# A hybrid decoder trunk on one core: the feed-forward norm reordered, its weight applied at PSUM exit, its sums moved off GpSimd, and the residual spread over eight down blocks

## The chip, the core and the metric

The kernel runs on one core of a Trainium2 chip. A core has five engines that run their own instruction queues side by side: TensorE (PE, matrix products; the loads of its stationary operand are shown as PEld), VectorE (DVE), ScalarE (ACT), GpSimd (POOL) and SyncE (SP), which here issues every DMA, in order. SBUF is the on-chip memory, PSUM the accumulator memory of PE, in eight banks for each of 128 partitions. The metric is the device time of one execution, in microseconds (us).

## The reference

Two layers; x is 1024 tokens by 1024 features, float32. What concerns the change is the second half of each layer:

```
D_MODEL, SEQ, D_FF, CONV_W = 1024, 1024, 2816, 3
def rms_norm(x, g):
    return x * rsqrt(mean(x * x, -1) + EPS) * g

for layer in range(2):
    h = rms_norm(x, norm_mix_g[layer])
    mix = even_mixer(...) if layer == 0 else gla_mixer(...)   # ends in  ... @ w_out
    x = x + mix
    h = rms_norm(x, norm_ffn_g[layer])
    g = causal_dwconv(h @ w_gate, conv_w, conv_b)             # width 3 along the tokens
    x = x + (silu(g) * (h @ w_up)) @ w_down
```

## The kernel before

Every product in question is made in three passes of a reduced float32 format (`fp32r`): a value is split into a high part (ACT casts it) and a low part (DVE subtracts the cast from the value), and `PASSES` multiplies high by high, high by low and low by high. `split(dst, src)` (lines 83 to 86) is that pair of instructions, and its rows in the profile carry lines 85 and 86 wherever it is called.

The 1024 tokens are eight tiles of 128 (`NT`). The normed activations are kept transposed (features on the partitions) in `hq[g][half]`: g is the parity of the feature block of 128, half the half of the tokens (tiles 0 to 3, or 4 to 7).

**Output projection and norm.** `out_first` makes the first 512 output columns for all tiles. `out_second` then makes the other 512, tile by tile: it loads the row tile `xt` (the first half from `xd`, where `out_first` put it, the second from the layer's input), `out_half` runs 24 products into a PSUM tile (`po`), adds them to the second half of `xt` on DVE (line 331) and writes that half to `xd` (line 332). `norm_tile` (line 118) follows for the same tile: ACT squares the row with a sum (line 123), POOL makes the inverse root (lines 114 and 115), DVE scales the row by it and by the norm weight `gB`, a copy of the weight on every partition, into a separate tile `h` (line 126), PE transposes `h` in eight blocks into PSUM (`pt`, line 135), and the result is split into `hq`.

**The feed-forward products** (`ffn_up`, line 192) use Strassen's scheme in Winograd's form on blocks: a stream is two feature blocks of gate or of up, and has seven products, steps 1 to 7, instead of eight. Their right operands are `hq[0][0]`, `hq[1][0]`, `hq[1][1]`, `hq[0][1]` for steps 1 to 4 and `T3[0]`, `T3[1]`, `T3[2]` for 5 to 7: differences of token halves, made once a layer. They need a tile of the second half with the tile four places before it, so they are made when tiles 4 to 7 are normed (lines 129 to 153): ACT copies the transposed blocks to `b`, POOL rebuilds the first half's values (`kept`, line 144), POOL and DVE make t1 to t4 (lines 145 to 148), and five splits follow. The left operands are sums of weight blocks, on POOL (`summed`, line 211), split like all others. The products go to PSUM tiles A, B and C (`pgA` for gate, `puA` for up, and so on); eight one-bank tiles (`m1`) are there. Steps 1 and 2 of the first two streams come first, then a loop over the streams makes steps 5, 6, 2, 7, the next stream's step 1, and 4 and 3. The depthwise convolution and SiLU follow on DVE and ACT, and the result goes to DRAM (`actd`).

**The down projection** (`ffn_down`, line 291) goes over blocks of two feature blocks (`FBLK`). Each block loads two activations and two weights into buffers of the pool `rawp` (four buffers of 512 KB for everything that is loaded raw), splits them, and runs 12 products of 512 columns for each token tile (`pd`, line 308); DVE adds them to the row tile `xs[n]` (line 318). The residual `xd` is loaded into the same pool and added (line 320) in one block of the eleven, for all eight tiles: `if fs[0] == NF // 4 * 2`, the sixth.

The order of each engine's instructions is fixed when the kernel is built: a planner takes the program in the order of the code and reorders each engine's queue by its own estimates of costs and due times. Buffers are given out tile by tile; an instruction that takes over a buffer waits for the last users of the old tile.

Of the kernel before, what the change touches and what calls it, by code (L numbers as in the profile page):

```python
# [51 lines left out]
def trunk(ctx: ExitStack, tc: tile.TileContext, a, out):  # L52
# [10 lines left out]
    small.tile([P, 8], F32, tag="pad", name="pad")  # L63
# [54 lines left out]
    def norm_tile(n, xt, gB, ps, pool, T3=None):  # L118


        h = pool.tile([P, D], F32, tag="h", bufs=2, name=f"h{n}")
# [3 lines left out]
        for _, c in HALVES:  # L125
            V.scalar_tensor_tensor(h[:, c], xt[:, c], r, gB[:, c], op0=ALU.mult, op1=ALU.mult)  # L126
        half, cols = n // 4, slice((n % 4) * P, (n % 4 + 1) * P)
        both = lambda t: [t[:, i, :, cols] for i in range(2)]
        if T3 and half:
            b = pool.tile([P, 2, 4, P], F32, tag="b", bufs=2, name=f"b{n}")  # L130
        for g in range(2):
            pt = ps.tile([P, 4, P], F32, tag="pt", name=f"pt{n}{g}")
            for j in range(4):
                k = 2 * j + g
                T.transpose(pt[:, j, :], h[:, k * P : (k + 1) * P], ident)  # L135
            if T3 and half:
                A.copy(b[:, g], pt)
            else:
                split(both(hq[g][half]), pt)
        if T3 and half:  # L140
            t1, t2, t3, t4 = (pool.tile([P, 4, P], F32, tag="tf", bufs=4, name=f"tf{n}{i}") for i in range(4))
            kept = [pool.tile([P, 4, P], F32, tag="kept", bufs=2, name=f"kept{n}{g}") for g in range(2)]
            for g in range(2):
                G.tensor_tensor(kept[g], *both(f32(hq[g][0])), op=ALU.add)
            G.tensor_tensor(t1, b[:, 0], kept[0], op=ALU.subtract)
            G.tensor_tensor(t3, b[:, 1], b[:, 0], op=ALU.subtract)
            V.tensor_sub(t2, b[:, 1], t1)
            V.tensor_sub(t4, kept[1], t2)
            split(both(T3[1]), t2)
            split(both(T3[0]), t1)  # L150
            split(both(T3[2]), t3)
            split(both(hq[0][1]), t4)
            split(both(hq[1][1]), b[:, 1])
# [38 lines left out]
    def ffn_up(l, T3, ps, pool):  # L192
# [6 lines left out]
        def stream(kind, f):  # L199
# [7 lines left out]
            sums, bank = {}, {}  # L207
# [16 lines left out]

            def step(p):
                L = parts_of(left(p), f"w{kind}{f}p{p}")
# [3 lines left out]
                if not more:  # L230
                    bank[b] = ps.tile([P, 512], F32, tag="m1", name=f"p{kind}{b}{f}")
# [20 lines left out]
            return step, out  # L252

        def conv(f, g2):
            ts = []
            for i in range(2):
                g = g2[:, i, :]
                t = pool.tile([P, S], F32, tag="t", bufs=3, name=f"t{f + i}")
                w = lambda j: cw[:, f + i, j : j + 1]
                A.activation(t, g, AF.Identity, bias=cb[:, f + i : f + i + 1], scale=w(2))  # L260
                V.scalar_tensor_tensor(t[:, 1:], g[:, : S - 1], w(1), t[:, 1:], op0=ALU.mult, op1=ALU.add)  # L261
                V.scalar_tensor_tensor(t[:, 2:], g[:, : S - 2], w(0), t[:, 2:], op0=ALU.mult, op1=ALU.add)  # L262
                A.activation(t, t, AF.Silu)  # L263
                ts.append(t)
            return ts
# [3 lines left out]
        for step, _ in (cur, nxt):  # L269
            step(1)  # L270
            step(2)
        for i, (kind, f) in enumerate(todo):
            step, out = cur
# [17 lines left out]
    def ffn_down(l, ps, pool, xs, final):  # L291
# [6 lines left out]
        def down(fs, last):  # L298
            acts = [act(f) for f in fs]
            wd = [load_w(a["w_down"][l, f], f"wd{f}") for f in fs]  # L300
            for n in range(NT):
# [15 lines left out]
                else:  # L317
                    V.tensor_add(xs[n], xs[n], flat(pd))  # L318
                    if fs[0] == NF // 4 * 2:
                        V.tensor_add(xs[n], xs[n], load_raw(xd[l][n], f"xd{l}{n}"))  # L320
# [7 lines left out]
    def out_half(l, half, wo, n, ps, xh):  # L328
        pd = ps.tile([P, 512], F32, tag="mm", name=f"po{half}{n}")
# [492 lines left out]
    for l in range(2):  # L822
# [59 lines left out]
def layouts(i):  # L882
# [21 lines left out]
    def ff(x):  # L904
# [8 lines left out]
        "norm_ffn_g": A["norm_ffn_g"],  # L913
# [37 lines left out]
```

## Time and profile before

| | us |
|---|---|
| median of 3 runs | 2363.51 (2362.66 to 2364.31) |
| profiled execution | 2365.36 |
| its span, first to last instruction | 2363.7 |
| PE busy | 2256.5 (95%) |
| DVE busy | 1388.8 (59%) |
| ACT busy | 890.2 (38%) |
| POOL busy | 486.9 (21%) |

The mean granted clock of PE is 0.979 of full speed. The first layer's second half of the output projection and its norm run from about 476 to 541 us of the span, gate and up from there to 972, down from 974 to 1223; the second layer's from about 1612, 1677 and 2110. A row of a timeline gives the start, the time from it to the end of the last instruction in the row, engine, line, operation, output and inputs, the count, and in brackets the idle time of the engine just before with what ended it. A row of groups gives a total and the mean in ns of one. A row of stretches gives each engine's busy time in the stretch.

### The profile page before, as it was taken

The numbers are of one execution on the slowest core, as the hardware profiler recorded it, in microseconds if no ns is written. First come the engines' busy times: TensorE is split into PE (matmuls) and PEld (weight loads), VectorE is DVE, ScalarE is ACT, GpSimd is POOL, SyncE is SP. The second block draws the span as 40 slices with busy tenths as digits, with TensorE's granted clock in tenths as the row PEclk, the third lists the DMA queues.
The fourth block names the chain that finished last, engine by engine and source line by source line (L and its number), as shares of the span: only waits on it lengthen the run. The fifth ranks groups of instructions, "written<-read, shape, count | busy, mean of one in ns | idle before, by whom it ended". The sixth has DMA issues, their size and how long they took to land.

```text
span 2363.7 us, 29172 instructions
## 1 busy us (share of the span) xinstructions
PE 2256.5 (95%) x11064; PEld 1912.0 (81%) x11064; DVE 1388.8 (59%) x2167; ACT 890.2 (38%) x1578; POOL 486.9 (21%) x535
## 2 busy tenths in 40 slices
PE   7999999988999999999999999999699999999999
PEld 7988877876888888787888888878588888878777
DVE  7666744458665655567664443244955655556674
ACT  5444554244443444511134333223444444442020
POOL 4333310036332332000000111001733323200000
PEclk9999999998999999999999999999799999999999
DMA  4122202341222222424232111454122222243241
GB/s 142 48 68 78 77 23 81 120 156 48 96 72 90 78 83 82 168 72 166 78 116 80 50 52 57 144 190 164 51 72 89 85 76 98 72 143 107 93 148 72
DMA packets 93309, 223.68 MB, mean 95 GB/s; under 512 B 10432, under 2 KB 35008, under 8 KB 93168
## 3 DMA queue, kind: packets, MB, share of 16 engines
q1 hardware_dynamic: 93168, 221.81, 28.1%
q8 instruction: 87, 1.43, 0.2%
q14 instruction: 54, 0.44, 0.1%
HBM read 167.18 MB, written 54.59 MB: 94 GB/s over the span
## 4 chain that ended last, share of the span: by engine, by line
PE 83%; DVE 8%; issue 3%; ACT 3%; DMA 2%; POOL 1%; SPq 0%; DVEq 0%; ACTq 0%; POOLq 0%
PE pd L308 19%; PE pgB L235 10%; PE puB L235 9%; PE po L171 6%; PE pgC L235 5%; PE pv L171 5%; PE puC L235 5%; PE pj L171 4%; PE pr L171 4%; PE pgA L235 2%; PE puA L235 2%; PE pk L183 2%; PE pq L183 2%; PE pu L171 1%; DVE T L86 1%
## 5 line engine op out<-in xcount | busy, mean ns | idle before, releaser
L308 PE MATMUL pd<-wd,act 128*128 128x512 f32 x2112 | 486.2, 392 | 14.5 <-ACT wd L85 9.7
L308 PEld LDWEIGHTS pd<-wd,act 128*128 128x128 f32 x2112 | 399.5, 189 | 100.4 <-ACT wd L85 14.7
L318 DVE TENSOR_TENSOR xr<-xr,pd 128x1024 f32<-128x1024 f32 x159 | 193.5, 1219 | 133.9 <-PE pd L308 133.3
L171 PE MATMUL po<-wo,hq 128*128 128x512 f32 x768 | 183.9, 394 | 2.2 <-ACT hq L349 1.3
L171 PEld LDWEIGHTS po<-wo,hq 128*128 128x128 f32 x768 | 141.7, 188 | 31.2 <-ACT hq L349 2.3
L171 PE MATMUL pv<-wv,hq 128*128 128x256 f32 (+2 forms) x960 | 155.5, 315 | 2.2 <-DVE gae L86 1.5
L171 PE MATMUL pj<-wq,hq 128*128 128x384 f32 x768 | 156.3, 351 | 1.3 <-ACT hq L85 1.3
L171 PEld LDWEIGHTS pv<-wv,hq 128*128 128x128 f32 x960 | 133.9, 191 | 11.0 <-DVE gae L86 1.7
L171 PEld LDWEIGHTS pj<-wq,hq 128*128 128x128 f32 x768 | 136.1, 195 | 2.0 <-ACT hq L85 1.7
L171 PE MATMUL pr<-wr,hq 128*128 128x512 f32 x384 | 97.9, 404 | 0.0
L287 DVE TENSOR_TENSOR t<-t,u 128x1024 f32<-128x1024 f32 x44 | 56.7, 1293 | 63.7 <-ACT u L248 63.7
L171 PEld LDWEIGHTS pr<-wr,hq 128*128 128x128 f32 x384 | 71.2, 188 | 14.5
L261 DVE SCALAR_TENSOR_TENSOR t<-g,cw,t 128x1023 f32<-128x1023 f32 x44 | 73.8, 1716 | 10.9 <-ACT t L260 10.9
L85 ACT CAST act<-ar 128x1024 fp32r<-128x1024 f32 x44 | 45.5, 1048 | 90.8 <-DMA ar<-actd 90.8
L135 PE MATMUL pt<-ident,h 128*128 128x128 f32 x256 | 40.8, 302 | 34.8 <-DVE h L126 26.0
L135 PEld LDWEIGHTS pt<-ident,h 128*128 128x128 f32 x256 | 33.0, 155 | 41.0 <-ACT h L123 16.1
L114 POOL TENSOR_SCALAR rn<-ssq 128x1 f32<-128x1 f32 x32 | 8.3, 261 | 264.8 <-ACT h L123 264.1
L263 ACT ACTIVATE t<-t 128x1024 f32<-128x1024 f32 x44 | 46.7, 1062 | 29.9 <-DVE t L262 29.8
L211 POOL TENSOR_TENSOR S2u<-S1u,ru 128x512 f32<-128x512 f32 x22 | 32.5, 1475 | 119.7 <-issue 113.0
L86 DVE TENSOR_TENSOR act<-ar,act 128x1024 fp32r<-128x1024 f32 x44 | 53.2, 1220 | 6.5 <-ACT act L85 6.4
L114 POOL TENSOR_SCALAR ro<-oss 128x1 f32<-128x1 f32 x32 | 9.8, 308 | 225.1 <-ACT og L765 225.1
L262 DVE SCALAR_TENSOR_TENSOR t<-g,cw,t 128x1022 f32<-128x1022 f32 x44 | 56.0, 1272 | 0.0
(920 smaller groups left out, 4716.9 us busy)
## 6 DMA issues: line engine op xcount, KB each, us to landing
rg<-in_w_gate SPq DMA_DIRECT2D x44, 512.0 KB, 3.6
ru<-in_w_up SPq DMA_DIRECT2D x44, 512.0 KB, 3.6
actd<-t SPq DMA_DIRECT2D x44, 512.0 KB, 2.6
ar<-actd SPq DMA_DIRECT2D x44, 512.0 KB, 4.2
xd<-xd SPq DMA_DIRECT2D x16, 512.0 KB, 4.3
x<-in_x SPq DMA_DIRECT2D x8, 512.0 KB, 5.3
xd<-xh SPq DMA_DIRECT2D x16, 256.0 KB, 2.0
xt<-xd SPq DMA_DIRECT2D x16, 256.0 KB, 3.1
```

Of the source, the lines that this page charges most:

```text
L85: (hi or A.copy)(dst[0], src)
L86: (lo or V.tensor_sub)(dst[1], src, f32(dst[0]))
L135: T.transpose(pt[:, j, :], h[:, k * P : (k + 1) * P], ident)
L171: T.matmul(o, L[i], R[jj][:, sl], start=(k == 0 and (ii, jj) == PASSES[0]), stop=(k == nk - 1 and (ii, jj) == PASSES[-1]))
L183: T.matmul(ps[h], L[i], hq[k % 2][h][:, jj, k // 2, :], start=(k == 0 and (ii, jj) == PASSES[0]), stop=(k == KD - 1 and (ii, jj) == PASSES ...
L235: T.matmul(o, L[ii][:, j * P : j * P + P], right[p][:, jj, j, :], skip_group_check=more, start=(not more and j == 0 and (ii, jj) == PASSES ...
L261: V.scalar_tensor_tensor(t[:, 1:], g[:, : S - 1], w(1), t[:, 1:], op0=ALU.mult, op1=ALU.add)
L262: V.scalar_tensor_tensor(t[:, 2:], g[:, : S - 2], w(0), t[:, 2:], op0=ALU.mult, op1=ALU.add)
L263: A.activation(t, t, AF.Silu)
L287: V.tensor_mul(ts[j], ts[j], out[:, j, :])
L308: T.matmul(pd[:, h, :], acts[k][:, i, n * P : (n + 1) * P], wd[k][h][jj], start=(k == 0 and (ii, jj) == PASSES[0]), stop=(k == len(fs) - 1 ...
L318: V.tensor_add(xs[n], xs[n], flat(pd))
```

## The change

`out_second` now takes the tiles in pairs, 0 4, 1 5, 2 3, 6 7; the row tiles of a pair are loaded into the buffers that later hold the gate and up outputs (tags `g` and `u`), and the scaled row overwrites the row tile (one `tensor_scalar` by the inverse root, no weight). The norm weight comes as one value for each partition and feature block (`gT`) and is applied when the transposed blocks leave PSUM: for tiles 0 to 3 by DVE, into `k`, which is kept for the partner tile and split into `hq`; for tiles 4 to 7 by eight multiplications on ACT, into `b`. t1 to t4 are made by DVE, and each is split at once. Tile 7's part after the scaling is handed to `ffn_up`, which calls it after steps 1 and 2 of the first stream and three early weight splits. The weight sums of the first two streams are made by DVE instead of POOL. `out_second` and `ffn_up` share one SBUF pool and one set of PSUM tiles: six `m1` (also for `po`) and two `pt`, which the transposes and the products A use. In the down projection, tile n's residual is added in block n + 1, counted from 0.

```
-    def norm_tile(n, xt, gB, ps, pool, T3=None):
+    def norm(n, xt, ps, h, gB=None):
         ssq = small.tile([P, 1], F32, tag="ssq", name=f"ssq{n}")
         A.activation(h, xt, AF.Square, accum_out=ssq)
         r = inv_rms(ssq, 1, D, f"rn{n}")
...
+        if gB is None:
+            h = xt
+            V.tensor_scalar(h, xt, r, None, op0=ALU.mult)
...
+        def turn(put):
             for g in range(2):
+                pt = ps.tile([P, 4, P], F32, tag="pt", name=f"pt{n}{g}")
+                for j in range(4):
+                    k = 2 * j + g
+                    T.transpose(pt[:, j, :], h[:, k * P : (k + 1) * P], ident)
+                put(g, pt)
+        return turn
...
             def summed(name, x, y, op):
-                sums[name] = pool.tile([P, 512], F32, tag="S", bufs=3, name=f"{name}{kind}{f}")
-                G.tensor_tensor(sums[name], x, y, op=op)
+                sums[name] = pool.tile([P, 512], F32, tag="S", bufs=4, name=f"{name}{kind}{f}")
+                (G if f else V).tensor_tensor(sums[name], x, y, op=op)
...
-                    bank[b] = ps.tile([P, 512], F32, tag="m1", name=f"p{kind}{b}{f}")
+                    bank[b] = ps.tile([P, 512], F32, tag="pt" if b == "A" else "m1", name=f"p{kind}{b}{f}")
...
-                t = pool.tile([P, S], F32, tag="t", bufs=3, name=f"t{f + i}")
+                t = pool.tile([P, S], F32, tag="t", bufs=4, name=f"t{f + i}")
...
-        for step, _ in (cur, nxt):
+        for step, _, _ in (cur, nxt):
             step(1)
             step(2)
+            if step is cur[0]:
+                for prep, p in ((nxt[2], 1), (nxt[2], 2), (cur[2], 5)):
+                    prep(p)
+                norm_end()
...
-                    if fs[0] == NF // 4 * 2:
+                    if fs[0] == FBLK * (n + 1):
                         V.tensor_add(xs[n], xs[n], load_raw(xd[l][n], f"xd{l}{n}"))
...
-    def out_second(l, w, x_in, g, T3, ps, pool):
+    def out_second(l, w, x_in, T3, ps, pool):
         wo = load_half(w[1], "wo1")
-        gB = load_g(pool, g, f"gBf{l}")
-        for n in range(NT):
-            xt = pool.tile([P, D], F32, tag="xt", bufs=2, name=f"xt{l}{n}")
-            Q.dma_start(xt[:, :512], xd[l][n][:, :512])
-            Q.dma_start(xt[:, 512:], x_in(n)[:, 512:])
-            out_half(l, 1, wo, n, ps, xt[:, 512:])
-            norm_tile(n, xt, gB, ps, pool, T3)
+        gT = small.tile([P, KD], F32, tag="gT", bufs=1, name=f"gT{l}")
+        Q.dma_start(gT, a["norm_ffn_gT"][l])
...
+        def temp(name):
+            return both(pool.tile([P, S], F32, tag="t", bufs=4, name=name))
+        def first(n, turn, k):
+            def put(g, pt):
+                gains = gT[:, g:KD:2, None].to_broadcast([P, 4, P])
+                V.tensor_tensor(k[:, g], pt, gains, op=ALU.mult)
+                split(place(hq[g][0], n), k[:, g])
+            turn(put)
+        def second(n, turn, k, b):
+            def put(g, pt):
+                for j in range(4):
+                    A.mul(b[:, g, j, :], pt[:, j, :], gT[:, 2 * j + g : 2 * j + g + 1])
+            turn(put)
+            t1, t2, t3, t4 = (F4(pool.tile([P, 512], F32, tag="S", bufs=4, name=f"tf{n}{i}")) for i in range(4))
+            V.tensor_sub(t1, b[:, 0], k[:, 0])
+            split(place(T3[0], n), t1)
+            V.tensor_sub(t2, b[:, 1], t1)
+            split(place(T3[1], n), t2)
+            V.tensor_sub(t3, b[:, 1], b[:, 0])
+            split(place(T3[2], n), t3)
+            V.tensor_sub(t4, k[:, 1], t2)
+            split(place(hq[0][1], n), t4)
+            split(place(hq[1][1], n), b[:, 1])
+        mine = {}
+        for i, pair in enumerate(((0, 4), (1, 5), (2, 3), (6, 7))):
+            xts = pool.tile([P, 2, S], F32, tag="gu"[i % 2], bufs=1, name=f"xt{l}{i}")
+            for j, n in enumerate(pair):
+                xt = xts[:, j]
+                Q.dma_start(xt[:, :512], xd[l][n][:, :512])
+                Q.dma_start(xt[:, 512:], x_in(n)[:, 512:])
+                out_half(l, 1, wo, n, ps, xt[:, 512:], "m1")
+                mine[n] = temp(f"n{n}")
+                turn = norm(n, xt, ps, mine[n].rearrange("p g a b -> p (g a b)"))
+                if n < 4:
+                    first(n, turn, mine[n])
+                elif n < 7:
+                    second(n, turn, mine[n - 4], mine[n])
+        return lambda: second(7, turn, mine[3], mine[7])
...
-            with tc.tile_pool(name=f"on{l}", bufs=1, reuse_waits="tile") as npool:
-                out_second(l, w_out, x_in, a["norm_ffn_g"][l : l + 1, :], T3, ps, npool)
             pss.close()
             with ExitStack() as st, tc.tile_pool(name=f"fu{l}", bufs=1, reuse_waits="tile") as fp:
-                ffn_up(l, T3, banks(st, m1=8), fp)
+                ps = banks(st, m1=6, pt=2)
+                norm_end = out_second(l, w_out, x_in, T3, ps, fp)
+                ffn_up(l, T3, ps, fp, norm_end)
```

More of the change, by code (lines that the diff above doesn't have):

```diff
@@ L124, in norm_tile @@
         r = inv_rms(ssq, 1, D, f"rn{n}")
[L125 to L139, printed above, removed]
@@ L140, in norm_tile @@
-        if T3 and half:
-            t1, t2, t3, t4 = (pool.tile([P, 4, P], F32, tag="tf", bufs=4, name=f"tf{n}{i}") for i in range(4))
-            kept = [pool.tile([P, 4, P], F32, tag="kept", bufs=2, name=f"kept{n}{g}") for g in range(2)]
-            for g in range(2):
[L144 to L153, printed above, removed]
+        if gB is None:
+            h = xt
+            V.tensor_scalar(h, xt, r, None, op0=ALU.mult)
+        else:
+            for _, c in HALVES:
+                V.scalar_tensor_tensor(h[:, c], xt[:, c], r, gB[:, c], op0=ALU.mult, op1=ALU.mult)
@@ new lines, in turn, with place, norm_tile @@
+        def turn(put):
+            for g in range(2):
+                pt = ps.tile([P, 4, P], F32, tag="pt", name=f"pt{n}{g}")
[4 more added lines that the diff above has]
+        return turn
+    def place(t, n):
+        return [t[:, i, :, (n % 4) * P : (n % 4 + 1) * P] for i in range(2)]
+    def norm_tile(n, xt, gB, ps, pool):
+        norm(n, xt, ps, pool.tile([P, D], F32, tag="h", bufs=2, name=f"h{n}"), gB)(
+            lambda g, pt: split(place(hq[g][n // 4], n), pt))
@@ L223, in left, with prep @@
                 return {1: A11, 2: A12, 4: A22}[p]
+            def prep(p):
+                made[p] = parts_of(left(p), f"w{kind}{f}p{p}")
             def step(p):
-                L = parts_of(left(p), f"w{kind}{f}p{p}")
+                if p not in made:
+                    prep(p)
+                L = made[p]
                 b = {2: "A", 5: "C", 3: "C"}.get(p, "B")
```

20 lines of the change are left out of this document (11 added, 9 removed).

## The prediction

> **What bounds the kernel now.** I read the page's busy shares and its chain first, to know whether TensorE (PE) is the bound; then the busy times by stretches, to find where PE is not busy; then the timelines of PE, VectorE (DVE) and the DMA queue (SP) in those stretches.
>
> ```profile
> PE 2256.5 (95%) x11064; PEld 1912.0 (81%) x11064; DVE 1388.8 (59%) x2167; ACT 890.2 (38%) x1578; POOL 486.9 (21%) x535
> PE 83%; DVE 8%; issue 3%; ACT 3%; DMA 2%; POOL 1%; SPq 0%; DVEq 0%; ACTq 0%; POOLq 0%
> ```
>
> PE sets the time nearly everywhere, so a change pays only where PE waits. Now the stretches:
>
> ```profile
> core 0: us, PE busy (x) PEld busy (x) DVE busy (x) ACT busy (x) POOL busy (x), PEclk, DMA share, GB/s
> 492.00:524.00 32.00, 32.00 (x166) 26.81 (x164) 18.19 (x25) 14.90 (x29) 10.32 (x15) 1.00 0.39 131
> 524.00:541.00 17.00, 4.05 (x16) 2.83 (x16) 17.00 (x18) 7.17 (x14) 13.06 (x10) 0.61 0.04 16
> 541.00:561.00 20.00, 13.65 (x53) 10.72 (x51) 19.21 (x19) 8.01 (x15) 11.98 (x8) 0.84 0.02 3
> 1081.00:1125.00 44.00, 39.21 (x160) 31.53 (x159) 36.40 (x35) 9.80 (x13) 0.00 (x0) 0.92 0.60 197
> 1661.00:1677.00 16.00, 3.80 (x15) 2.66 (x16) 16.00 (x17) 6.33 (x12) 12.07 (x10) 0.60 0.04 16
> 1677.00:1697.00 20.00, 13.85 (x52) 11.05 (x51) 19.21 (x19) 7.84 (x15) 12.15 (x8) 0.84 0.02 2
> ```
>
> From 524 to 561 PE is idle for 12.95 + 6.35 = 19.3 us while DVE has no idle time to speak of (17.00 of 17.00, 19.21 of 20.00). That is the end of the feed-forward norm. The second layer repeats it at 1661: 12.2 + 6.15 = 18.35 us in these two stretches. Around 1100, in the down projection, PE loses 4.8 us more. PE's own rows in the norm:
>
> ```profile
> 531.71 1.09 PE L135 MATMUL pt<-ident,h 128*128 128x128 f32 x4 [7.63 <-DVE h L126]
> 533.97 1.12 PE L135 MATMUL pt<-ident,h 128*128 128x128 f32 x4 [1.17 <-DVE h L126]
> 538.74 1.09 PE L135 MATMUL pt<-ident,h 128*128 128x128 f32 x4 [3.66 <-ACT T L85]
> 540.32 1.11 PE L135 MATMUL pt<-ident,h 128*128 128x128 f32 x4 [0.49 <-DVE h L126]
> 541.09 4.68 PE L235 MATMUL pgB<-hq,wg0p 128*128 128x512 f32 x12
> 548.35 2.88 PE L235 MATMUL puB<-hq,wu0p 128*128 128x512 f32 x12
> 560.30 5.32 PE L235 MATMUL pgC<-T,wg0p 128*128 128x512 f32 x12 [6.34 <-ACT wg0p L85]
> 966.36 3.02 PE L235 MATMUL puB<-hq,wu20p 128*128 128x512 f32 x12 [0.90 <-ACT u L245]
> 498.16 1.03 PE L135 MATMUL pt<-ident,h 128*128 128x128 f32 x8
> 498.95 5.70 PE L171 MATMUL po<-wo,hq 128*128 128x512 f32 x24
> ```
>
> The transposes of tiles 6 and 7 wait for their scaled rows, and the fifth product (pgC) for its weights, whose sum sat behind the tile work on POOL. The stalls also slow what follows: a group of twelve takes 4.68 and 5.32 us behind them and 2.88 otherwise (granted clock 0.61 and 0.84 in these stretches), 1.8 + 2.4 us lost. Sixteen transposes take 4.1 us there (1.09 + 1.12 + 1.09 + 0.77 to the next start); where PE is fed, eight take 0.8 us to the next start, so 2.5 us are lost. Together 19.3 + 4.2 + 2.5 = **26 us a layer** is the most that the norm can give back.
>
> Why DVE is late there:
>
> ```profile
> 536.47 1.58 POOL L145 TENSOR_TENSOR tf<-b,kept 128x512 f32<-128x512 f32 x1 [2.13 <-ACT hq L85]
> 538.01 1.71 POOL L146 TENSOR_TENSOR tf<-b 128x512 f32<-128x512 f32 x1
> 536.85 3.42 DVE L126 SCALAR_TENSOR_TENSOR h<-xt,rn,gBf 128x512 f32<-128x512 f32 x2
> 508.19 1.41 DVE L126 SCALAR_TENSOR_TENSOR h<-xt,rn,gBf 128x512 f32<-128x512 f32 x2 [1.16 <-POOL rn L115]
> 540.19 1.75 DVE L148 TENSOR_TENSOR tf<-kept,tf 128x512 f32<-128x512 f32 x1
> 541.87 0.68 DVE L86 TENSOR_TENSOR hq<-b,hq 128x512 fp32r<-128x512 f32 x1
> 542.47 2.37 DVE L86 TENSOR_TENSOR T<-tf,T 128x512 fp32r<-128x512 f32 x2
> 494.31 1.28 DVE L86 TENSOR_TENSOR hq<-pt,hq 128x512 fp32r<-128x512 f32 x2
> 485.50 0.69 DVE L331 TENSOR_TENSOR xt<-xt,po 128x512 f32<-128x512 f32 x1 [8.36 <-DMA xt<-in_x]
> 488.32 1.41 DVE L126 SCALAR_TENSOR_TENSOR h<-xt,rn,gBf 128x512 f32<-128x512 f32 x2 [0.83 <-POOL rn L115]
> ```
>
> The two scalings take 1.41 us by themselves and 3.42 us beside POOL's sums; a subtraction takes 0.68 (the next starts after 0.60) or about 1.75. All four Strassen tiles (4 to 7) come last, so this work piles up behind the last output product.
>
> **The change part by part.** *POOL's sums go (four for each of tiles 4 to 7, two more to rebuild kept), DVE takes them at 0.60.* DVE's rows lose the slow form. Of POOL only the 128x1 steps remain, and the weight sums of all streams but the first two.
>
> *DVE's new sum* to the moment that the fifth product needs: tiles 0 to 3 cost one add (0.60), one scaling, two multiplications with the weight at PSUM exit and two split subtractions (4 x 0.64, half of the 1.28 that two take from PSUM). The in-place scaling, 128x1024 with one scalar, is not in the trace; the nearest rows are these:
>
> ```profile
> L762 DVE TENSOR_SCALAR st<-us,dec 128x256 f32<-128x256 f32 x28 | 9.9, 353 | 0.8
> L426 DVE TENSOR_SCALAR gv<-gv,mv,lr 128x512 f32<-128x512 f32 x8 | 4.4, 546 | 6.0 <-POOL lr L115 6.0
> L551 ACT COPY vN<-pj 128x128 f32<-128x128 f32 x32 | 8.2, 261 | 21.8 <-PE po1n L522 6.0 <-DVE qn L548 5.4 <-PE po3n L522 4.6
> xd<-xt SPq DMA_DIRECT2D x16, 256.0 KB, 2.8
> ```
>
> From 353 at 256 to 546 at 512 elements, 1024 come to 0.93 us; the bounds are 0.55 (no longer than 512) and 1.41 (the two it replaces). So 4 x (0.60 + 0.93 + 2.56) = 16.4. Tiles 4 to 7 cost an add, a scaling and nine of 0.60: 4 x 6.93 = 27.7, less the seven of tile 7 that the fifth product does not need (4.2): 23.5. Beside them five weight splits, the sum S1 (DVE's for the first two streams now) and two adds into the output: 8 x 0.60 = 4.8. Sum 44.7 us. From the first add at 485.50, which waits for its row load now too, plus 2.7 us of first latency (scaling about 489.4, two adds in between), DVE could be there at 533.
>
> *PE's side.* Its products are the same; in the order 0 4 1 5 2 3 6 7 the Strassen work of 4 and 5 lies beside output products. The first products of gate and up (four of 2.72 us) need tiles 0 to 3 alone, so gate's two now stand ahead of tile 7's transposes, and up's two behind. Without any stall the fifth product starts at 560.30 + 2.4 - 26 = 536.7. Tile 7's own chain: last output product done 524.1 (531.71 - 7.63), add 0.69, write and scaling 3.1 + 0.93, transposes 0.8, eight ACT multiplications of 0.26 (2.1), a subtraction, a cast taken as long, a subtraction (3 x 0.68): 533.8. Both arrive before 536.7, with 3 us to spare.
>
> *What eats that.* The scaling in place is a new wait: the output half is written to DRAM from the same rows (2.8 us from issue to landing, 3.1 with the issue). Now a scaling starts 2.13 us after its add has ended (486.19 to 488.32). So the wait adds 1.0 us a tile, 8 us a layer if nothing else is ready on DVE, 0 if the queue always has something. The split subtractions and adds behind it on DVE are queued, and PE's transposes wait for it. The write itself is queued on SP behind the loads for a later pair, which wait for a pair's buffer. Also the Square of tiles 2, 3, 6, 7 now lands in a buffer that the tiles two places ahead must have left. I take 5 us of PE stall a layer, nearer the whole wait than none since DVE is filled to nine tenths (11.0 us a pair, where PE takes 2 x (24 x 0.227 + 0.8) = 12.5), plus 2 us of slow clock behind it: **7 us of the 26 stay, 19 to 20 come back.** Bounds: 0 to 26 come back. Twice 19.5 = 39.
>
> [...]
>
> *m1 of six banks and pt of two* in place of eight: three banks a stream, two streams in flight, six of eight; costed at nothing, since DVE empties A within a stream's 7 x 2.72 = 19 us. Four sums more per stream on DVE in the first two streams: 8 x 0.60 in 27 us of PE, hidden. The weight load ahead of the rows shrinks from a copy for each partition to one: counted as nothing, since PE is fed until 524 either way.
>
> *Residual in eight down blocks.* Now eight residual loads stand in one block on SP:
>
> ```profile
> 1045.86 50.77 SPq L90 DMA_DIRECT2D xd<-xd x8
> 1099.03 3.04 SPq L90 DMA_DIRECT2D ar<-actd x2
> 973.80 130.84 PE L308 MATMUL pd<-wd,act 128*128 128x512 f32 x576 [1.70 <-DVE u L250]
> 1108.97 11.17 PE L308 MATMUL pd<-wd,act 128*128 128x512 f32 x36 [4.33 <-ACT wd L85]
> 1120.60 90.99 PE L308 MATMUL pd<-wd,act 128*128 128x512 f32 x400 [0.46 <-DVE xr L318]
> 2246.36 10.81 PE L308 MATMUL pd<-wd,act 128*128 128x512 f32 x36 [5.34 <-ACT wd L85]
> 2258.10 100.98 PE L308 MATMUL pd<-wd,act 128*128 128x512 f32 x444 [0.94 <-DVE xr L318]
> ```
>
> They hold the four raw buffers and the queue for 50.77 us, each waiting for its tile's add; the next block's activations are asked for at 1099, 5.6 us before PE needs them (973.80 + 130.84 = 1104.6). It loses 4.33 + 0.46 us, and 36 products take 11.17 where 36 x 0.227 = 8.2 is the rate (90.99 / 400): 2.9. Sum 7.7; in the second layer 5.34 + 0.94 + 2.5 = 8.8. With one load a block, four loads of the next block share three buffers for part of a block; a block is 96 x 0.227 = 21.8 us and loads run two blocks ahead elsewhere (576 products without a gap), so the one buffer less is covered. The added 1.2 us of DVE for one tile of a block fits its 2.72. **16.5 us come back**; bounds 0 and 16.5.
>
> Sum: 39 + 16.5 = 55.5 us. The profiled execution had a span of 2363.7 and took 2365.36; the median is 2363.51, and I subtract there: **2308 us**, 2.3% less.
>
> **The rivals.** *All comes back (0.13):* DVE's 533 holds. 2363.5 - 52 - 16.5 = 2295. For it: the 3 us to spare; against: an order fixed ahead, on a DVE nine tenths full.
>
> *DVE stays the bound through the in-place wait (0.23).* If half of 3.1 us is uncovered at each of eight scalings, 12.4 us go on top of 533: 545.4, 9 us late, and 4 of slow clock: 13 of 26 come back, 2363.5 - 26 - 16.5 = 2321. With all of it uncovered, 24.8: 558, next to nothing comes back, up to 2345. For it: the DMA engines are 0.39 busy from 492 to 524, so a write can meet loads; against: the scaling can stand behind other ready work. [...]
>
> *Slower (0.06).* One mechanism: on SP the write of a tile stands behind the load of a later pair that waits for the buffer, so each tile runs one after another. Serial, tiles 0 to 3 cost 0.69 + 3.1 + 0.93 + 0.8 + 2.56 = 8.1 and 4 to 7 0.69 + 3.1 + 0.93 + 0.8 + 2.1 + 5.4 + 0.68 = 13.7: 87 us, less 4.2, from 485.5: 568, against 562.7 now; with 16.5 gained below that is still 2358. It ends slower by 0.2% where a write takes over 3.7 us from its add, and at 5 us each it gives 583 and 2388. Against it: six banks let PE run other tiles' products meanwhile, and two pairs have buffers of their own.
>
> *The residual gains nothing (0.04):* the held buffer starves some block: 2324. *Nothing moves (0.03):* both gains are eaten, about 2361.
>
> **How the numbers follow.** My case, 2299 to 2320, has 0.51. The range 2293 to 2338 takes in full recovery and most of the second rival and leaves out some 0.12. A measurement of this kernel tells about 0.2% (4.7 us) from no change. Faster: 0.51 + 0.13 + 0.23 + 0.04 = 0.91; same 0.03; slower 0.06.
>
> **What would show it.** After: POOL nearly idle in both norms; DVE's subtractions all near 0.68; gate's first two groups directly behind the last output product; stalls ahead of the fifth product of 5 us in place of 19; the scaling's releaser named as a DMA write; no stall on down weights and no 50 us stretch of residual loads. The forecast is wrong if PE's transposes wait in the middle of the output products, which it does nowhere from 492 to 524 now, or if a new stall shows within the feed-forward products.

## The result, and the profile after

The changed kernel takes 2324.26 us (2323.97 to 2325.47) against 2363.91 for the kernel before on the same chip: 39.7 us less, ratio 0.9834, 95% interval 0.9817 to 0.9851. The forecast was 55.5 us less. The profiled execution took 2324.36 us, with a span of 2322.4.

From the page of the changed kernel, the busy shares, the chain that ended last and the group of the down products:

```profile
PE 2249.0 (97%) x11064; PEld 1906.8 (82%) x11064; DVE 1363.9 (59%) x2199; ACT 901.7 (39%) x1626; POOL 412.3 (18%) x487
PE 84%; DVE 6%; ACT 3%; DMA 3%; issue 3%; POOL 1%; SPq 0%; DVEq 0%; ACTq 0%; POOLq 0%
L310 PE MATMUL pd<-wd,act 128*128 128x512 f32 x2112 | 479.8, 389 | 4.2 <-DVE u L248 4.2
```

TensorE is at 97% and in the chain VectorE is down from 8% to 6%. Of the down products only 4.2 us of waiting is left, for the last `u` of the stream and not for weights or the residual.

PE's timeline dates the stages, so the span can be cut into six stretches, in us: to the end of the last `pc` transposes of `out_first`; from there to the first `pd` product (second output half, norm, gate and up); down; and the same for layer 1.

| kernel | 1 | 2: norm, gate, up | 3: down | 4 | 5: norm, gate, up | 6: down | span |
|---|---|---|---|---|---|---|---|
| before | 464.6 | 509.2 | 249.4 | 377.4 | 509.5 | 253.5 | 2363.7 |
| after | 462.1 | 497.1 | 241.3 | 379.2 | 498.6 | 244.2 | 2322.4 |
| difference | -2.5 | -12.2 | -8.2 | +1.8 | -11.0 | -9.3 | -41.3 |

Stretches 1 and 4 hold nothing that the change touches, and over all the kernels below they ran from 462.1 to 468.7 and from 376.6 to 380.0. Together they make 840.7 to 847.5 us, so a whole time carries up to 7 us that have nothing to do with an edit; a difference of under 2 us in a stretch is read as none. So the residual gave 17.5 us (forecast 16.5) and the norm 12.2 and 11.0 us (forecast 19.5 each).

What is left in the norm of layer 0: the stretches of the changed kernel, with the engines' busy times, PE's granted clock, DMA share and GB/s.

```profile
core 0: us, PE busy (x) PEld busy (x) DVE busy (x) ACT busy (x) POOL busy (x), PEclk, DMA share, GB/s
490.00:520.00 30.00, 30.00 (x152) 25.18 (x151) 21.55 (x35) 18.60 (x43) 3.36 (x8) 1.00 0.34 112
520.00:541.00 21.00, 16.65 (x73) 13.24 (x72) 17.99 (x30) 13.85 (x34) 3.40 (x4) 0.84 0.05 17
520.00:528.00 8.00, 3.88 (x21) 3.21 (x20) 7.79 (x13) 4.74 (x10) 3.20 (x4) 0.76 0.11 42
541.00:561.00 20.00, 17.31 (x67) 13.21 (x66) 17.09 (x28) 9.49 (x18) 6.73 (x4) 0.91 0.32 105
548.30:552.20 3.90, 3.89 (x11) 3.09 (x12) 3.90 (x7) 1.49 (x4) 0.00 (x0) 0.60 0.67 201
900.00:959.20 59.20, 55.56 (x244) 45.03 (x242) 38.16 (x44) 30.08 (x44) 7.71 (x5) 1.00 0.27 93
1080.00:1104.00 24.00, 24.00 (x108) 19.87 (x107) 16.33 (x17) 4.18 (x6) 0.00 (x0) 1.00 0.35 122
```

PE is idle for 4.35 + 2.69 = 7.0 us from 520 to 561, where it was idle for 19.3 before. Its clock is still down there; busy time by what the clock lacks of 1 gives, as an estimate, 16.65 x 0.16 + 17.31 x 0.09 = 4.2 us lost. In the down projection (1080 to 1104) it has no gap. Its timeline names the waits:

```profile
520.61 0.60 PE L136 MATMUL pt<-ident,xt 128*128 128x128 f32 x4
522.31 0.66 PE L136 MATMUL pt<-ident,xt 128*128 128x128 f32 x4 [1.11 <-DVE n L376]
525.98 1.97 PE L136 MATMUL pt<-ident,xt 128*128 128x128 f32 x8 [3.01 <-DVE n L376]
528.60 3.79 PE L233 MATMUL pgB<-hq,wg0p 128*128 128x512 f32 x11
541.71 0.39 PE L233 MATMUL pgC<-T,wg0p 128*128 128x512 f32 x1
546.55 0.73 PE L233 MATMUL pgB<-T,wg0p 128*128 128x512 f32 x2 [1.47 <-ACT wg0p L85]
548.31 4.00 PE L233 MATMUL pgB<-T,wg0p 128*128 128x512 f32 x10 [1.02 <-DVE wg0p L86]
959.16 229.67 PE L310 MATMUL pd<-wd,act 128*128 128x512 f32 x1012 [2.10 <-DVE u L248]
2078.19 239.64 PE L310 MATMUL pd<-wd,act 128*128 128x512 f32 x1056 [2.10 <-DVE u L248]
```

There are two pairs of stalls. The first (1.11 + 3.01 us) is at the transposes of tiles 3 and 6, which wait for VectorE to take the earlier transposes out of PSUM with the gain (L376). The second (1.47 + 1.02 us) is behind the fifth product, at the weights of the sixth. The fifth product itself (pgC, 541.71) no longer waits. Layer 1 shows the same four waits (1.06, 3.01, 1.47 and 1.02 us). VectorE's timeline around the first pair:

```profile
486.88 1.51 DVE L126 TENSOR_SCALAR xt<-xt,rn 128x1024 f32<-128x1024 f32 x2 [2.53 <-DMA xd<-xt]
502.59 0.75 DVE L126 TENSOR_SCALAR xt<-xt,rn 128x1024 f32<-128x1024 f32 x1 [1.56 <-DMA xd<-xt]
512.89 0.76 DVE L126 TENSOR_SCALAR xt<-xt,rn 128x1024 f32<-128x1024 f32 x1 [2.39 <-ACT n L384]
522.18 0.68 DVE L86 TENSOR_TENSOR wu0p<-ru,wu0p 128x512 fp32r<-128x512 f32 x1
522.77 0.74 DVE L126 TENSOR_SCALAR xt<-xt,rn 128x1024 f32<-128x1024 f32 x1
523.44 0.68 DVE L86 TENSOR_TENSOR wu0p<-ru,wu0p 128x512 fp32r<-128x512 f32 x1
524.04 0.68 DVE L86 TENSOR_TENSOR hq<-n,hq 128x512 fp32r<-128x512 f32 x1
524.64 0.68 DVE L333 TENSOR_TENSOR xt<-xt,po 128x512 f32<-128x512 f32 x1
525.24 1.28 DVE L376 TENSOR_TENSOR n<-pt,gT 128x512 f32<-128x512 f32 x2
545.16 0.69 DVE L204 TENSOR_TENSOR S2g<-S1g,rg 128x512 f32<-128x512 f32 x1
547.57 0.69 DVE L86 TENSOR_TENSOR wg0p<-S2g,wg0p 128x512 fp32r<-128x512 f32 x1
```

VectorE is idle ahead of five of the eight in-place scalings, 7.9 us in all; the three longest pieces are shown, and two of them, 2.53 + 1.56 = 4.1 us, were ended by the row write. In layer 1 the row write ended one piece, of 1.6 us. From 520 to 528 VectorE is full (7.79 of 8.00): the two multiplications that PE waits for at 525.24 stand behind weight splits, a scaling and an add. And between the sum S2 (545.16) and its split (547.57), which the sixth product needs, stand S3, a split and S4.

### The profile page after: what moved, and what is told of

Its sections match the earlier page's. It is cut to its first block, busy times and chain, and to the rows that moved or that the text cites. A ratio compares the mean times of both kernels' runs of the same rounds, so it can differ in the third digit from the quotient of the medians.

```text
span 2322.4 us, 29094 instructions
## 1 busy us (share of the span) xinstructions
PE 2249.0 (97%) x11064; PEld 1906.8 (82%) x11064; DVE 1363.9 (59%) x2199; ACT 901.7 (39%) x1626; POOL 412.3 (18%) x487
## 3 DMA queue, kind: packets, MB, share of 16 engines
q8 instruction: 87, 1.43, 0.2%
## 4 chain that ended last, share of the span: by engine, by line
PE 84%; DVE 6%; ACT 3%; DMA 3%; issue 3%; POOL 1%; SPq 0%; DVEq 0%; ACTq 0%; POOLq 0%
PE pd L310 21%; PE pgB L233 11%; PE puB L233 10%; PE pv L164 5%; PE puC L233 5%; PE pgC L233 5%; PE po L164 5%; PE pj L164 4%; PE pr L164 4%; PE pgA L233 3%; PE puA L233 2%; PE pk L176 2%; PE pq L176 2%; PE pu L164 1%; PE pt L136 1%
## 5 line engine op out<-in xcount | busy, mean ns | idle before, releaser
L310 PE MATMUL pd<-wd,act 128*128 128x512 f32 x2112 | 479.8, 389 | 4.2 <-DVE u L248 4.2
L164 PE MATMUL pu<-wu,hq 128*128 128x512 f32 x192 | 51.8, 416 | 1.3 <-ACT ut L488 1.3
L258 ACT ACTIVATE t<-g,cb,cw 128x1024 f32<-128x1024 f32 x44 | 52.3, 1238 | 0.8
L204 POOL TENSOR_TENSOR S4g<-rg,S2g 128x512 f32<-128x512 f32 x20 | 25.8, 1291 | 130.1 <-DVE wu2p L86 18.6
```

The source lines that it names most:

```text
L164: T.matmul(o, L[i], R[jj][:, sl], start=(k == 0 and (ii, jj) == PASSES[0]), stop=(k == nk - 1 and (ii, jj) == PASSES[-1]))
L310: T.matmul(pd[:, h, :], acts[k][:, i, n * P : (n + 1) * P], wd[k][h][jj], start=(k == 0 and (ii, jj) == PASSES[0]), stop=(k == len(fs) - 1 ...
```

## The experiments

The accounting below is the same for each kernel, in layer 0: PE's idle time in the 37 to 41 us of the norm's end, what the clock lacks there (in the kernel before up to 600 us), and PE's idle time in the last stretch before the down products. The last of these is 3.6 us in the changed kernel, 59.20 - 55.56. The kernel before adds these rows to those shown:

```profile
561.00:600.00 39.00, 39.00 (x165) 31.94 (x164) 30.15 (x31) 20.78 (x33) 22.29 (x14) 0.95 0.26 81
900.00:973.80 73.80, 71.20 (x313) 58.32 (x312) 46.21 (x55) 35.52 (x54) 12.84 (x9) 1.00 0.31 102
```

| kernel | idle | slow clock | idle before down | sum | less than before | stretch 2, less than before |
|---|---|---|---|---|---|---|
| before | 19.3 | 1.6 + 2.2 + 1.9 | 2.6 | 27.6 | | |
| after | 7.0 | 2.7 + 1.6 | 3.6 | 14.9 | 12.7 | 12.2 |
| write wait gone (e3) | 5.1 | 0 | 3.6 | 8.7 | 18.9 | 17.6 |
| half in place (e8) | 4.6 | 1.5 | 3.6 | 9.7 | 17.9 | 17.0 |
| and sums early (e9) | 3.5 | 0 | 2.6 | 6.1 | 21.5 | 21.2 |

The sums meet the measured stretches within 1.3 us, so these three columns are where the time is. Each row is one profiled execution; those of e3 and e8 are the longest of their four runs.

**The two halves apart (e1, e2).** The kernel before with the residual edit alone, and the changed kernel with the old residual:

```diff
-  if fs[0] == NF // 4 * 2:
+  if fs[0] == FBLK * (n + 1):     # e1, in before; e2 is the reverse, in after
```

> The kernel before with one line changed: tile n's residual is added in down block n + 1 instead of all eight in the sixth block. If the down stall is a matter of eight loads holding the four raw buffers (my theory): 16 to 18 us less than before, about 2346.5, no wait of PE on down weights, and the norm as before. Rival, that the stall is one of DMA bandwidth or returns elsewhere: less than 8 us.

> The changed kernel with the residual back in the sixth block. If the parts simply add: 22 to 24 us less than before, about 2341, with the down stall of 7.7 and 8.8 us back. Rival, that the norm part helps the down projection or is helped by it: the two parts alone do not add up to 39.7 us, by more than 3 us.

The residual alone took 2351.07 us (ratio 0.9944, 0.9929 to 0.9959), 13.1 us less than before, which is under the 16 to 18 expected. Its two down stretches, 241.3 and 245.8, were 15.9 us shorter, and the stretches that it does not touch 1.5 us longer; PE waited for no down weights. The norm alone took 2345.29 (0.9923, 0.9904 to 0.9941), 18.9 us less, under the 22 to 24 expected, with 9.9 and 11.5 us less in stretches 2 and 5 and the waits on down weights back. By whole times the halves give 13.1 + 18.9 = 32.0 of the 39.7 us, by stretches 15.9 + 21.3 = 37.2 of the 40.6 that the change took from the same four. Both fall short by more than the 3 us that were set for the rival, so that the parts simply add is not shown. The norm's half gave 21.3 of the 39 us forecast for it, so the shortfall of the change is there.

**The write wait (e3).** The second output half is written to DRAM from the rows that it was loaded into, and no longer from the rows that are scaled. It leaves out the mixer's part of these columns in the residual.

```diff
-  out_half(l, 1, wo, n, ps, xt[:, 512:], "m1")
+  out_half(l, 1, wo, n, ps, xt[:, 512:], "m1", x_in(n)[:, 512:])   # rows that the write reads
   ...                                                              # out_half takes them as src
```

> The changed kernel, but the second half of the residual row goes to DRAM from the layer's input instead of from the row tile, so that the scaling in place no longer waits for that write; the DMA traffic stays, and the residual lacks the mixer's part of those columns. Theory A (the write wait is what keeps 11 us of stall a layer; VectorE waited for it 4.1 and 1.6 us): 4 to 12 us faster than the changed kernel, 2312 to 2320. Theory B (VectorE's amount and order of work from 513 us on is what keeps it, and the early waits are idle time that is made up): within 2 us of 2324.

2318.15 us (0.9801, 0.9784 to 0.9817); stretches 2 and 5 are 5.5 and 5.8 us shorter than in the changed kernel. VectorE's waits at the scaling (what, for whom, us in total, times, longest), in the second fence the stretches around PE's former stall, and in the third PE's rows at the sixth product:

```profile
DVE xt L126 <- POOL rn L115: 8.0, 4, 2.1
```

```profile
525.00:545.00 20.00, 17.98 (x89) 14.21 (x88) 18.54 (x31) 15.19 (x36) 2.17 (x4) 1.00 0.01 1
545.00:565.00 20.00, 16.91 (x72) 12.83 (x71) 17.31 (x24) 9.82 (x18) 8.25 (x6) 1.00 0.33 106
```

```profile
548.06 0.73 PE L233 MATMUL pgB<-T,wg0p 128*128 128x512 f32 x2 [1.43 <-ACT wg0p L85]
549.82 2.58 PE L233 MATMUL pgB<-T,wg0p 128*128 128x512 f32 x10 [1.03 <-DVE wg0p L86]
```

The scaling now waits for the row's norm and not for a write, PE is idle for 2.02 + 3.09 us, and the clock stays at 1.00. But VectorE waits as long at the scalings as in the changed kernel, 8.0 us against 7.9. What differs is the rest of its queue: without the write the planner puts the first scaling (491.52) ahead of the second tile's add (492.19), where in the changed kernel that add (483.67) stands ahead of the first scaling (486.88). From the first add to the first of the two multiplications that PE waited for, VectorE takes 43.3 us in the changed kernel, 12.9 of them idle, and 39.8 in e3, 9.9 of them idle. And some 1.5 us of the gain in layer 0 is not the write's: the two stalls at the sixth product are the same as in the changed kernel, but the ten products behind them took 2.58 us instead of 4.00, at a clock of 1.00 instead of 0.60. So a kernel in which no write stands ahead of the scaling is 5.5 and 5.8 us faster in the two layers, and of the 5.5 about 4 go with the write; whether by the wait itself or by the order that the planner makes because of it, this run does not separate.

**VectorE's amount (e4).** Tiles 2 and 3 get the gain by eight ScalarE multiplications each, as tiles 4 to 7 do.

```diff
-  V.tensor_tensor(k[:, g], pt, gains, op=ALU.mult)
+  if n < 2: V.tensor_tensor(k[:, g], pt, gains, op=ALU.mult)
+  else:
+      for j in range(4): A.mul(k[:, g, j, :], pt[:, j, :], gT[...])
```

> The changed kernel, with the norm weight of tiles 2 and 3 applied by eight multiplications on ScalarE, as tiles 4 to 7 have it, instead of two on VectorE. Theory B (VectorE full and its order): 2.4 us of VectorE work go from each layer's full stretch and the transposes' PSUM tiles are freed by ScalarE: 5 to 12 us faster than the changed kernel, 2312 to 2319, and the 1.1 and 3.0 us waits of PE on those multiplications go. Theory A (the write wait): within 2 us of 2324.

2328.14 us (0.9846, 0.9831 to 0.9860), stretches +1.8 and -0.4: nothing. On PE's timeline one wait was put in place of another:

```profile
528.12 0.66 PE L136 MATMUL pt<-ident,xt 128*128 128x128 f32 x4 [3.49 <-ACT n L380]
```

PE waits as long (3.9 us in two pieces), now for ScalarE, which takes 2.2 us for eight multiplications where VectorE took 1.28 for two. The 5 to 12 us of the theory that VectorE has too much to do did not come. But the run took work off VectorE by putting a longer step into the same chain, so it does not tell what less work on VectorE is worth by itself.

**The weight sums back on POOL, for all streams (e5).**

```diff
-  (G if f else V).tensor_tensor(sums[name], x, y, op=op)
+  G.tensor_tensor(sums[name], x, y, op=op)
```

> The changed kernel, with the weight sums of the first two streams back on GpSimd. VectorE loses eight additions a layer (4.8 us) but works beside GpSimd again, where a subtraction took 1.75 us in place of 0.68. If the neighbour costs more than the additions (theory of the shared cost): the stretch from the second half of the output products to the down projection grows by 1 to 5 us a layer over 497.1 and 498.6. Rival, that VectorE's amount of work alone counts: it shrinks by 2 to 5 us a layer.

2331.55 us (0.9868, 0.9851 to 0.9884), stretches +2.3 and +3.4. On VectorE's timeline two weight splits beside POOL's sums, of 0.69 us in the changed kernel:

```profile
551.61 1.77 DVE L86 TENSOR_TENSOR wg0p<-rg,wg0p 128x512 fp32r<-128x512 f32 x1
553.30 1.76 DVE L86 TENSOR_TENSOR wg0p<-S4g,wg0p 128x512 fp32r<-128x512 f32 x1
```

So this part of the change is worth some 3 us a layer. Whether by VectorE's longer splits or by POOL's own sums, which took 1.5 to 1.7 us each there, the run does not separate.

**The first products late (e6).** The Strassen work of tile 7 is issued ahead of the first products, as the kernel before had it.

```diff
-  return lambda: second(7, turn, mine[3], mine[7])
+  second(7, turn, mine[3], mine[7])
+  return lambda: None
```

> The changed kernel, with tile 7's part directly behind its scaling in the program, ahead of all first products and weight splits. If the first products early are what covers tile 7's chain: 3 to 8 us more a layer in that stretch (over 497.1 and 498.6). Rival, that the planner sets the queues by readiness whatever the order of the code: within 1.5 us.

2326.15 us (0.9839, 0.9823 to 0.9855), stretches +1.6 and -1.3: no effect, as the rival had it. Where these products stand in the program is not worth anything that the run can tell.

**The order of the tiles (e7, e11, e12).** First 0 4 1 5 2 6 3 7; then 0 1 2 3 4 5 6 7, which needs five `t` buffers, so a control has these buffers with the order of the change.

```diff
-  for i, pair in enumerate(((0, 4), (1, 5), (2, 3), (6, 7))):
+  for i, pair in enumerate(((0, 4), (1, 5), (2, 6), (3, 7))):   # e7
+  for i, pair in enumerate(((0, 1), (2, 3), (4, 5), (6, 7))):   # e11, with t 5, S 3, s1 1 buffers; e12: these alone
```

> The changed kernel with the pairs 0 4, 1 5, 2 6, 3 7. Tile 3, which the first products need, comes seventh in place of sixth, and two Strassen tiles come after each other no more than before. If the cover by first products matters: 2 to 7 us more a layer in that stretch. Rival, that only the total of VectorE's work and its waits count: within 1.5 us.

> The control with the tiles in their own order, pairs 0 1, 2 3, 4 5, 6 7, so that the four Strassen tiles come last again, as in the kernel before; all else as in the control. If the interleaved order is what keeps VectorE from piling up behind the last output product: 5 to 12 us more a layer in that stretch than the control. Rival, that the gain of 12 us a layer is made by the sums that left GpSimd and the rest (the runs that put a part of them back cost 1 to 3 us): within 2 us of the control.

> Control for the next run: the changed kernel with five buffers of 1024 columns (tag t) in place of four, three of 512 (S) in place of four, and one s1 in place of two, which takes the same room. All theories: the stretch from the second half's products to the down projection stays within 2 us of 497.1 and 498.6.

The first took 2326.13 us (0.9841, 0.9826 to 0.9856), stretches +0.8 and -0.5: no difference. The order in turn took 2328.48 (0.9846, 0.9832 to 0.9861) and its control 2323.79 (0.9828, 0.9812 to 0.9844); against the control its stretches are 3.6 and 3.1 us longer, between the two expectations, and the medians differ by 2.3 us a layer. But the scaling also waits longer for the write in it. VectorE's waits in layer 0, in the order in turn and in its control:

```profile
DVE xt L126 <- DMA xd<-xt: 9.6, 3, 5.9
```

```profile
DVE xt L126 <- DMA xd<-xt: 1.9, 1, 1.9
```

So the order in turn costs 2 to 3.5 us a layer, and that this is for the Strassen tiles' place and not for the longer waits is not shown. Which pair stands third is not worth anything that these runs can tell.

**Half of the rows in place (e8).** The half that the write reads is scaled into a buffer of its own; the half that was written long before is scaled in place.

```diff
-  V.tensor_scalar(xt, xt, r, None, op0=ALU.mult)
+  h2 = small2.tile([P, 512], F32, tag="s1", bufs=2, name=f"hh{n}")
+  V.tensor_scalar(xt[:, :512], xt[:, :512], r, None, op0=ALU.mult)
+  V.tensor_scalar(h2, xt[:, 512:], r, None, op0=ALU.mult)
   ...                                                      # the transposes read xt and h2
```

> The changed kernel with the full result, but only the first half of a row is scaled in place; the second half, which is being written to DRAM, is scaled into a buffer that stands free until the first stream (two of 512 columns). One VectorE instruction more a tile, and no scaling waits for the write. If the write wait is the cause of the 5.5 us a layer that the run without it gained: that stretch goes to 491 to 493 us in each layer, 2311 to 2316 in all. Rival, that the run without it gained by another order of the queues: within 2 us of 497 and 498.6.

2315.64 us (0.9790, 0.9773 to 0.9808), stretches 4.9 and 3.7 us shorter than in the changed kernel: 492.2 as expected, and 494.8, above the 493 expected. That agrees with e3 without its 1.5 us of clock. VectorE's queue again has the first scaling (487.21) ahead of the second tile's add (488.01), and takes 40.1 us (9.4 idle) from the first add to those multiplications, so e8 does not exclude its rival, another order of the queues. What is left, on VectorE's timeline, on PE's, and in the stretches:

```profile
487.21 0.49 DVE L126 TENSOR_SCALAR xt<-xt,rn 128x512 f32<-128x512 f32 x1 [2.13 <-POOL rn L115]
542.27 0.68 DVE L207 TENSOR_TENSOR S2g<-S1g,rg 128x512 f32<-128x512 f32 x1
545.28 0.68 DVE L86 TENSOR_TENSOR wg0p<-S2g,wg0p 128x512 fp32r<-128x512 f32 x1
```

```profile
543.65 0.73 PE L236 MATMUL pgB<-T,wg0p 128*128 128x512 f32 x2 [1.31 <-ACT wg0p L85]
546.01 3.89 PE L236 MATMUL pgB<-T,wg0p 128*128 128x512 f32 x10 [1.63 <-DVE wg0p L86]
```

```profile
520.00:541.00 21.00, 19.32 (x95) 15.50 (x94) 19.97 (x35) 16.52 (x40) 1.99 (x4) 1.00 0.07 26
541.00:561.00 20.00, 17.06 (x67) 13.28 (x67) 13.80 (x24) 8.50 (x16) 6.88 (x5) 0.91 0.34 106
```

The sixth product waits for the split of S2, which comes 3.0 us after the sum, and ten products behind the two stalls take 3.89 us. Up to 541 PE now idles 1.68 us at a full clock; the 2.94 us and the clock of 0.91 behind that are this second pair of stalls.

**The weight sums of gate early (e9).** In the kernel of e8, the operands of the sixth and seventh product are made together with that of the fifth.

```diff
-  for prep, p in ((nxt[2], 1), (nxt[2], 2), (cur[2], 5)):
+  for prep, p in ((nxt[2], 1), (nxt[2], 2), (cur[2], 5), (cur[2], 6), (cur[2], 7)):
```

> The kernel with the second half scaled into the free buffer, and with the weight sums and splits of gate's steps 6 and 7 placed ahead of tile 7's part, as step 5's is. In that kernel PE waited 1.31 and 1.63 us in step 6 for the split of S2, which VectorE made 3.0 us after the sum, behind three later sums. If the order of VectorE's queue is what is left: 2 to 3 us less a layer in the stretch from the second half's products to the down projection (492.2 and 494.8 to 489 to 492), about 2311. Rival, that VectorE is simply full there until 552 us: the wait moves to T3 of tile 7 and nothing is gained (within 1.5 us a layer).

2308.04 us (0.9757, 0.9744 to 0.9771): the fastest of all. Stretches 2 and 5 are 4.2 and 5.6 us shorter than in e8, more than the 2 to 3 expected. VectorE and PE at the sixth product, and the stretches with the last before the down products, a fence each:

```profile
533.12 0.69 DVE L207 TENSOR_TENSOR S2g<-S1g,rg 128x512 f32<-128x512 f32 x1
536.13 0.69 DVE L86 TENSOR_TENSOR wg0p<-S2g,wg0p 128x512 fp32r<-128x512 f32 x1
```

```profile
543.13 2.66 PE L236 MATMUL pgB<-T,wg0p 128*128 128x512 f32 x11
```

```profile
520.00:540.00 20.00, 16.97 (x83) 13.13 (x81) 19.88 (x35) 15.84 (x39) 1.98 (x4) 1.00 0.06 22
540.00:560.00 20.00, 19.52 (x86) 15.96 (x87) 14.59 (x23) 9.06 (x17) 11.48 (x6) 1.00 0.33 103
900.00:951.30 51.30, 48.70 (x214) 39.73 (x213) 34.08 (x41) 27.37 (x40) 4.25 (x3) 1.00 0.32 106
```

S2's split is done 6 us ahead of its product, PE is idle for 3.03 + 0.48 us, and the clock is 1.00 throughout. Beside 1.1 us of stall, the slow clock behind it (1.5 us) and 1.0 us before the down products went too, which makes up most of the 4.2. The 5.6 of layer 1 is not accounted for in this way. That 2308 is also what was forecast for the change is chance: this is another kernel.

**Two of the tiles' sums on POOL (e10)**, t1 and t3, as in the kernel before.

```diff
-  V.tensor_sub(t1, b[:, 0], k[:, 0])
+  G.tensor_tensor(t1, b[:, 0], k[:, 0], op=ALU.subtract)     # t3 likewise
```

> The changed kernel with t1 and t3 of the four Strassen tiles on GpSimd, as before the change. VectorE loses eight subtractions a layer (4.8 us); GpSimd took 1.3 to 1.7 us for each, and VectorE's neighbours took up to 1.75 us in place of 0.68. If VectorE's cost beside GpSimd is what the change took away: 2 to 8 us more a layer in that stretch than 497.1 and 498.6. Rival, that the gain came from the interleaved order alone: within 1.5 us a layer.

2332.62 us (0.9860, 0.9844 to 0.9875), but stretches 2 and 5 only +1.1 and +1.2. That is within the rival's 1.5 us and not told from nothing; the rest of the time lies in stretches that the edit does not touch.

## Why the prediction was right, and where it was off

*Where the time is, and its sign:* right. PE was the bound, the time came back at the norm's end and at the residual's block, and POOL is out of the norm but for the 128x1 steps.

The time itself, 2324.3, lies outside the prediction's own case (2299 to 2320, chance 0.51), in the part of its range that was there for the rivals.

*The residual:* right, 16.5 us forecast, 17.5 here and 15.9 in e1. Without the 50 us block of loads in the four raw buffers PE waited for no down weights.

*The durations:* close. The scaling takes 0.75 us (estimated 0.93), subtractions 0.68. The eight ScalarE multiplications, estimated at 2.1 us:

```profile
511.73 2.16 ACT L384 ACTIVATE n<-pt,gT 128x128 f32<-128x128 f32 x8
```

Beside POOL's sums a split took 1.77 us in e5, against 0.69. The six banks of `m1` cost nothing that shows. For a `pt` tile to come free PE waits at 522 and 526; two of them were costed at nothing, and no run had more.

*The cover by the first products:* the work was there, but its place in the program was not what gave it (e6), nor was it the third pair's order (e7). Gate's first groups do stand behind the last output products, though after two stalls.

*What eats the gain:* the step that failed. It put 5 us of PE stall and 2 us of slow clock on each layer, and had 26 us as the most to win. Measured in layer 0: 7.0 us of stall, 4.2 of slow clock, 1.0 of new idle time before the down products, and 25.0 to win (19.3 + 5.7). That is 2.0 + 2.2 + 1.0 + 1.0 = 6.2 of the 7.3 us by which 19.5 was missed; 0.5 is the step from 26 - 7 = 19 to 19.5, and 0.6 stays open. Up to 541 us, before the fifth product, the size was right: 4.35 us of stall and 2.7 of slow clock, 7.0 in all. What failed is that the sum ended there: the 2.7 us of stall, 1.6 of slow clock and 1.0 of idle time behind the fifth product had no term, since VectorE's sum was counted only to what the fifth product needs. The places differ too. There was no wait of 5 us ahead of the fifth product, but four short ones: two between the last output product and gate's first, and two at the sixth product. The latter are the new stall within the feed-forward products that the prediction had named as a sign against it.

*The two causes.* That a write stands ahead of the scaling costs about 4 us a layer (4.3 by e8, 5.6 by e3 with 1.5 of clock), and the order of the sixth product's sums another 4.9 (e9). The first shows as a wait for PSUM: the multiplications that free the `pt` tiles come late in VectorE's fixed queue, at 525.24, behind splits that PE does not yet need. In layer 0 the chain that ended last runs three times through a row write to the scaling that waits for it, 4.45 + 1.99 + 1.99 us. Removing the write in two ways shows that the cost goes with it; how much of it is the wait and how much the planner's other order stays open.

*The fifth product* was put at 536.7 without any stall, so at 543.7 with the 7 us that the sum took; it began at 541.71, or 544.2 with 2.5 us for the earlier end of stretch 1.

*The rivals:* DVE the bound through the in-place wait (2321) was the nearest, in time and in mechanism, though what was lost was about half to the write and half to the sums' order. The slower rival did not occur: the tiles do not run one after another. Its mechanism did, once in layer 0: on SP the fourth tile's write was issued 1.0 us after its add had ended (497.0), behind loads for a later pair. It also took long, as the chain that ended last shows:

```profile
498.02 4.45 DMA xd<-xt
```

Together that is 5.5 us, and the first tile's write took 4.1; both are more than the 3.7 us from which that rival would have decided, but for two tiles and not for eight. The writes of layer 0 landed 2.0 to 4.5 us after their issue, five of the eight within 2.2.

*The clock:* the 2 us of slow clock in the sum were the author's estimate, against 4.2 worked out from the clock of layer 0. The clock fell to 0.76 around pieces of 1.11 and 3.01 us, and to 0.60 behind 1.47 and 1.02 us, where ten products took 4.00 us; from 560.78, at a clock of 1.00, ten took 2.43. In e9, with waits of 1.30, 1.23 and 0.98 us further apart, it stayed at 1.00. But the size of the pieces does not decide by itself, for in e3 the pair of 1.43 and 1.03 us left the clock of layer 0 at 1.00, with 2.58 us for the ten products. What decides it is not shown by these runs. Nor are the 1.5 us between e3 and e8 a merit of the write's removal: in e8 no scaling waits for the write either, and its pair, of 1.31 and 1.63 us, was followed by 3.89 us.

*Open:* undone one at a time, the order in turn (3.4 us, with longer waits for the write in it), the sums on POOL (2.9), t1 and t3 on POOL (1.1, not told from nothing) and the products' place (0) make at most 7.4 of the 11.6 us a layer that the norm gained. The rebuilding of `kept` on POOL and the weight at PSUM exit were not tried alone.

## What to carry to other kernels

Before scaling rows in place, look for a transfer that still reads them; here a buffer of half the size for the part still being written brought 9 us. A wait on an engine with a fixed queue need not show its price where it stands: here the cost that goes with VectorE's waits for the row write (4.1 us in layer 0) came out as a stall of PE at the transposes (1.11 + 3.01 us), with a clock of 0.76 around it. Taking a dependency away also lets the planner make another order, so such a run measures both. And when a stall is costed up to the operand that is late, cost the next operands too: putting their sums ahead brought as much again (4.2 and 5.6 us in e9, after 4.9 and 3.7 in e8).

## What the hardware showed that was not expected

A scaling of 128x1024 takes VectorE 0.75 us and one of 128x512 0.49, so one instruction is cheaper than two halves; the halves won all the same. Two stalls of 1.47 and 1.02 us with two products between them were followed by 3.9 us at a clock of 0.60, and nearly the same two (1.43 and 1.03) in e3 by a full clock: there ten products took 2.58 us in place of 4.00. Why is not shown.
